# Last down projection as seven products of Strassen's form

## The chip, the cores and the metric

The kernel runs on one core of a Trainium2 chip. A core has a matrix engine (TensorE, PE in the profile; its weight loads are PEld), a vector engine (VectorE, DVE), a scalar engine (ScalarE, ACT), a general engine (GpSimd, POOL) and a sync engine (SyncE, SP) that issues the transfers here. Each has a queue of its own that runs in order. Sixteen DMA engines carry the transfers. SBUF is the working memory; PSUM has eight banks of 128 x 512 float32 in which matmuls accumulate. The metric is the time of one execution on the device in microseconds (us), by the median of several.

## The reference, cut to what matters

Two layers over 1024 tokens of 1024 channels, in float32. Each layer is a token mixer and then a gated feed-forward with a short causal convolution. The change touches the last matrix product of the second layer.

```
D_MODEL = 1024; SEQ = 1024; FFN_DIM = 2816; FFN_CONV_WIDTH = 3
def conv_ffn(h, w_up, w_dw, b_dw, w_down):
    u = h @ w_up
    u = causal_dwconv(u, w_dw) + b_dw
    gate, val = jnp.split(u, 2, axis=-1)
    return (jax.nn.silu(gate) * val) @ w_down
...
    for i in range(DEPTH):
...
        h = rms_norm(x, ffn_norm_g[i])
        x = x + conv_ffn(h, ffn_w_up[i], ffn_w_dw[i], ffn_b_dw[i], ffn_w_down[i])
```

The down projection multiplies a 1024 x 2816 matrix (tokens by channels, called the activations below) by a 2816 x 1024 weight.

## The kernel before, in words

**Precision.** A float32 operand is split into a high part (a cast, L347, on ACT) and a low part (the operand minus the high part, L348, on DVE or POOL). `mm3` (L350) makes a product of three matmuls: high by high, high by low, low by high, at L353, L355 and L354. High and low parts stand in tiles `whi` and `wlo`, eight buffers each (`SPLIT_BUFS`, L46).

**Pieces.** The work is a stream of `Piece` objects (L62): each may have a load, a split and a run (its matmuls or adds). `trace` (L259) writes them out: loads as far ahead as eight `raw` buffers allow, splits as long as the tiles of split pieces that have not run stay within `READY + 1` = 6 (a down piece has 2). The frame then orders each engine's queue by its own model of times, except PE's, which keeps the order of the pieces in this stage (`T.order(PE)`, in `ffn_up`, L1402). Waits between engines come from the data and from buffers that are used again.

**The up stage of the second layer** (`up`, L538) already computes its products in Strassen's form, as 2 x 2 blocks over halves of tokens, channels and columns. For each of 22 channel tiles f it runs products over PSUM banks y and z; the conv taps (L580), the gate (L589) and sums over blocks (L558 on POOL; L628, L638, L639, L643, L652 on DVE) follow. The result, 128 channels x 1024 tokens, is stored to `actd[f]` in HBM. Its factors stand in quarters of 128 x 4 x 512 (`quarter`, L156), eight in the pool `ht` and six in `late`.

**The down stage** (`down`, L408, called by `down_acts`, L691, and `ffn_down`, L1429) runs over the two halves h of the tokens and, in each, the two halves nh of the columns. For each of these four blocks it takes four PSUM banks (128 tokens x 512 columns each) and goes over the 22 channel tiles: a piece loads `actd[f]` for 512 tokens and 512 columns of the weight's rows, 256 KB each, splits both, and makes 4 x 3 matmuls of 128 x 512. After the 22 pieces a piece adds the four banks to the residual (L435), and after the second half of the columns a row block of 128 x 1024 is stored to the output (`out`, L1506). That is 88 pieces and 1056 matmuls. The residual is fetched from HBM after the fourth piece (`fetch_x`, L1296). The first two down pieces stand between the last up pieces (`STOP` in `up`).

**Buffers near the change.** `bank` (L505) takes one of six PSUM banks; two more are in the pool `pst`. `part` (L405) takes one of 14 tiles of 128 x 512.

Of the kernel before, what the change touches and what calls it, by code (L numbers as in the profile page):

```python
# [9 lines left out]
F32 = mybir.dt.float32  # L10
# [3 lines left out]
ALU = mybir.AluOpType  # L14
# [3 lines left out]
P = 128  # L18
# [7 lines left out]
NF = F // P  # L26
# [3 lines left out]
def f32(ap):  # L30
    return ap.bitcast(F32)
# [13 lines left out]
RAW_BUFS = 8  # L45
# [27 lines left out]
class Weight:  # L73
# [6 lines left out]
    def load(self):  # L80
        if self.raws:
            self.raw = self.t.load(self.src, self.shape)

    def split(self):
        t = self.t
        if not self.raws:
            self.parts = tuple(
                t.wp.tile(self.shape, F32R, tag=m, name=t.n(m), bufs=SPLIT_BUFS) for m in ("whi", "wlo")
            )
            for part, src in zip(self.parts, (self.hi, self.lo)):  # L90
                t.nc.sync.dma_start(f32(part), src)
# [21 lines left out]
class Trunk:  # L113
# [577 lines left out]
    def down_acts(self, xs, l, h, actd, w_down, after, los=None, actlo=None):  # L691


        def act(f, w):
            src = actd[f][:, h * 512 : (h + 1) * 512]
            if actlo and f in actlo:
                return Weight(self, None, [P, 512], actlo[f], hi=src)
            return Weight(self, src, [P, 512], vector=w.lo is None)

        rows = [w_down[l, f * P : (f + 1) * P, :] for f in range(NF)]  # L700
        for nh in range(2):
            yield from self.down(xs, h, nh, act, rows, after if nh == 1 else None, los)


    def attn(self, wst0, x_in, gain, w_in, b_f, q_g, k_g, extra=lambda *a: None, early=lambda: None):
# [599 lines left out]
def trunk(ctx, tc, a):  # L1305
    nc = tc.nc
    T = Trunk(ctx, tc)
# [32 lines left out]
    actd = [dram.tile([P, S], F32, name=f"actd{f}") for f in range(NF)]  # L1340
    xds = [[dram.tile([P, D], F32, name=f"xd{i}_{t}") for t in range(NB)] for i in range(3)]
# [4 lines left out]
    xs = [None] * NB  # L1346
# [36 lines left out]
    def turned(gen, n=1):  # L1383

        for i in range(6):
            yield T.norms(int(i < 4), int(1 <= i < 5), int(i >= 2))
            yield from some(gen, (1 if i else LAG) * n)
# [14 lines left out]
    def ffn_up(l, keep, first, then, late, fac, ups, held=()):  # L1402


        keep["vector"] = True
        if late:
            yield from turned(first)
        combine = T.combine(fac, keep)
        for _ in range(6):
            yield from some(combine, 1)  # L1410
            yield from some(first, 1 if late else 2)
        for i in range(6):
            yield from some(combine, 1)
            yield from some(first, 1)
            if i >= 6 - BEFORE:
                if held:
                    yield held.pop(0)
                else:
                    yield from some(ups, 1)
        keep["stop"] = True  # L1420
        yield from first
        yield T.order(PE)
        for p in ups:
            if p is STOP:
                yield from some(then, 1)
            else:
                yield p

    def ffn_down(l, h, xd, after, los=None, actlo=None):  # L1429
        for i, p in enumerate(T.down_acts(xs, l, h, actd, a["ffn_w_down"], after, los, actlo)):  # L1430
            yield p
            if i == 3:
                yield Piece(lambda: T.fetch_x(xs, xd, h))

    keep = {"xd": xds[0]}
# [17 lines left out]
    for ct in range(KT):  # L1453
        for s in range(2):
            for q in range(2):
                c0 = s * D + ct * P
                src = w_pw1.rearrange("(k p) n -> p k n", p=P)[:, 4 * q : 4 * q + 4, c0 : c0 + P]
                T.ahead.append(lambda src=src, lo=pwlo[2 * ct + s][q]: T.split_ahead(src, lo))
    for f in range(NF):
        for nh in range(2):  # L1460
            src = a["ffn_w_down"][0, f * P : (f + 1) * P, nh * 512 : (nh + 1) * 512]
# [7 lines left out]
    keep1 = {"xd": xds[2]}  # L1469
# [33 lines left out]
        return T.conv(xs, xds[1], h, hc, w_pw1, pwlo, taps, vec, a["conv_w_pw2"][0], halo,  # L1503
                      normer(grows, keep1, True))

    def out(tb):  # L1506
        nc.sync.dma_start(a["out"][0, tb * P : (tb + 1) * P, :], xs[tb])

    PE = mybir.EngineType.PE

    def pieces():
        conv_rows = ((grows, a["conv_norm_g"][0]), (b2, a["conv_b_pw2"][0]))
        yield T.order()
        down0 = ffn_down(0, 0, xds[0], conv_norm)
        yield from ffn_up(0, keep, T.early(0, keep, w_up), down0, False, *ups_of(0, keep))
        yield T.order()
        for r in conv_rows:
            yield fetch(*r)
        while (yield from some(down0, ASIDE)):
            if T.ahead:  # L1520
                yield T.ahead.pop(0)()
        down1 = ffn_down(0, 1, xds[0], conv_norm, dnlo, actlo)
        yield from turned(down1)
        main0, norm0, rest0 = conv(0)
        yield from main0([down1])
        yield from some(down1, 3)
        yield from some(norm0, 1)
        yield from some(down1, 3)
        yield from both(norm0, down1, 1, 2)
        for r in conv_rows:  # L1530
            yield fetch(*r)
# [12 lines left out]
        yield from turned(main1, 2)  # L1544
        first = T.early(1, keep1, w_up)
        fill.append(first)
        yield from main1
        yield T.order()
        keep1["vector"] = True
        yield from some(first, 5)  # L1550
        yield from some(norm1, 1)
        yield from some(first, 3)
        keep1["hold"] = True
        while keep1["begun"]:
            yield from some(norm1, 1)
            yield from some(first, 1)
        keep1["hold"] = False
        yield fetch(grows, a["ffn_norm_g"][1])
        fac, ups = ups_of(1, keep1)
        held = []  # L1560
        yield from norm1
        yield from some(rest1, 8)
        for p in itertools.islice(ups, 3):
            ahead, then = T.apart(p)
            yield ahead
            held.append(then)
        yield from rest1
        downs = [ffn_down(1, h, xds[2], out) for h in range(2)]
        yield from ffn_up(1, keep1, first, downs[0], True, fac, ups, held)
        for d in downs:  # L1570
            yield from d

    T.trace(pieces())


# [23 lines left out]
```

## Time and profile before

| what | us |
|---|---|
| median of three runs | 2324.36 |
| lowest and highest | 2323.95, 2328.08 |
| the profiled execution, by the device | 2321.22 |
| its span, first to last instruction | 2319.5 |
| first matmul of the last down projection | 2068.1 |
| its last matmul starts | 2312.7 |

The profile is of one execution. A row of a group shows an engine, an operation, the tiles it writes and reads, and its busy time. Where three numbers stand with slashes, they are the least, the median and the greatest duration in nanoseconds. In a timeline a row begins with the start and the duration in us, and a bracket shows how long the engine was idle before it and what ended that. Rows by stretches of the span show the busy time of each engine in each. PE's matmuls overlap: a matmul of 128 x 512 is shown with 389 ns, but one starts every 227 ns.

### The profile page before, as it was taken

The numbers are of one execution on the slowest core, as the hardware profiler recorded it, in microseconds if no ns is written. First come the engines' busy times: TensorE is split into PE (matmuls) and PEld (weight loads), VectorE is DVE, ScalarE is ACT, GpSimd is POOL, SyncE is SP. The second block draws the span as 40 slices with busy tenths as digits, with TensorE's granted clock in tenths as the row PEclk, the third lists the DMA queues.
The fourth block names the chain that finished last, engine by engine and source line by source line (L and its number), as shares of the span: only waits on it lengthen the run. The fifth ranks groups of instructions, "written<-read, shape, count | busy, mean of one in ns | idle before, by whom it ended". The sixth has DMA issues, their size and how long they took to land.

```text
span 2319.5 us, 35294 instructions
## 1 busy us (share of the span) xinstructions
PE 2252.0 (97%) x11282; PEld 1927.3 (83%) x11282; DVE 1648.1 (71%) x2751; ACT 1358.0 (59%) x2835; POOL 1406.7 (61%) x1191
## 2 busy tenths in 40 slices
PE   7899999998999999999999999998999999999998
PEld 7899999997878887777787887787877788888887
DVE  6567777777367999998436995699639999983222
ACT  5566666667255666666545665566635666664443
POOL 3445555535017988886554886677536999955543
PEclk9999999999999999999999999999999999999999
DMA  5222222134155546666878767654564554566664
GB/s 146 65 78 83 78 78 78 57 127 166 66 178 188 154 151 207 198 200 199 300 250 296 249 226 263 217 185 142 166 202 154 156 154 150 154 224 208 221 202 153
DMA packets 366841, 392.63 MB, mean 169 GB/s; under 512 B 26416, under 2 KB 245312, under 8 KB 366656
## 3 DMA queue, kind: packets, MB, share of 16 engines
q1 hardware_dynamic: 366656, 390.38, 53.2%
q8 instruction: 89, 1.46, 0.3%
q14 instruction: 96, 0.79, 0.1%
HBM read 299.78 MB, written 82.12 MB: 165 GB/s over the span
## 4 chain that ended last, share of the span: by engine, by line
PE 47%; DVE 17%; issue 4%; ACT 3%; DMA 1%; POOL 1%; SPq 0%; DVEq 0%; ACTq 0%; POOLq 0%
DVE acc L580 8%; PE dn L354 7%; PE dn L355 7%; PE dn L353 7%; PE pw L353 2%; PE pw L354 2%; PE pw L355 2%; PE e L353 2%; PE e L355 2%; PE e L354 2%; PE y L353 2%; PE y L354 1%; PE y L355 1%; ACT acc L584 1%; PE wops L353 1%
## 5 line engine op out<-in xcount | busy, mean ns | idle before, releaser
L348 POOL TENSOR_TENSOR wlo<-raw,whi 128x512 fp32r<-128x512 f32 (+1 forms) x306 | 444.8, 1456 | 275.2 <-ACT whi L347 239.3
L347 ACT CAST whi<-raw 128x512 fp32r<-128x512 f32 (+2 forms) x497 | 303.2, 633 | 263.9 <-PE dn L354 154.3
L348 DVE TENSOR_TENSOR wlo<-raw,whi 128x512 fp32r<-128x512 f32 (+1 forms) x191 | 149.3, 784 | 228.0 <-ACT whi L347 207.9
L348 POOL TENSOR_TENSOR wlo<-s,whi 128x512 fp32r<-128x512 f32 x176 | 258.8, 1480 | 64.1 <-ACT whi L347 64.1
L353 PE MATMUL dn<-whi,whi 128*128 128x512 f32 x704 | 275.7, 392 | 1.0 <-ACT whi L347 0.6
L354 PE MATMUL dn<-wlo,whi 128*128 128x512 f32 x704 | 274.6, 390 | 0.8 <-POOL wlo L348 0.8
L355 PE MATMUL dn<-whi,wlo 128*128 128x512 f32 x704 | 274.4, 390 | 0.0
L1182 DVE SCALAR_TENSOR_TENSOR cacc<-u,ctaps,cacc 128x512 f32<-128x512 f32 x320 | 238.6, 754 | 9.0
L1187 POOL TENSOR_TENSOR pacc<-pacc,prod 128x512 f32<-128x512 f32 x144 | 188.9, 1314 | 50.1 <-ACT prod L1186 43.8
L353 PE MATMUL y<-bhi,whi 128*128 128x512 f32 x528 | 207.6, 393 | 7.7 <-DVE u L638 5.2
L355 PE MATMUL y<-bhi,wlo 128*128 128x512 f32 x528 | 205.8, 390 | 0.0
L354 PE MATMUL y<-blo,whi 128*128 128x512 f32 x528 | 205.6, 389 | 0.0
L169 POOL TENSOR_SCALAR ss<-ss 128x4 f32<-128x4 f32 (+1 forms) x96 | 22.9, 238 | 289.9 <-ACT hn L189 150.2
L353 PE MATMUL pj<-whi,hthi 128*128 128x384 f32 (+1 forms) x512 | 177.8, 348 | 4.6 <-DVE zf L824 2.6
L355 PE MATMUL pj<-whi,htlo 128*128 128x384 f32 (+1 forms) x512 | 177.2, 346 | 0.0
L354 PE MATMUL pj<-wlo,hthi 128*128 128x384 f32 (+1 forms) x512 | 176.2, 344 | 0.7 <-DVE wlo L348 0.7
L558 POOL TENSOR_TENSOR s<-raw,raw 128x512 f32<-128x512 f32 x88 | 126.4, 1436 | 59.5 <-DMA c11d<-ev 58.2
L914 POOL TENSOR_SCALAR x<-x,nm 128x896 f32<-128x896 f32 (+7 forms) x128 | 101.4, 797 | 100.1 <-DVE nm L913 72.3
L353 PEld LDWEIGHTS dn<-whi,whi 128*128 128x128 f32 x704 | 132.5, 188 | 29.5 <-issue 1.1
L354 PEld LDWEIGHTS dn<-wlo,whi 128*128 128x128 f32 x704 | 132.6, 188 | 28.9 <-POOL wlo L348 1.2
L355 PEld LDWEIGHTS dn<-whi,wlo 128*128 128x128 f32 x704 | 132.5, 188 | 27.4
L584 ACT ACTIVATE acc<-acc 128x512 f32<-128x512 f32 x88 | 55.7, 632 | 163.3 <-DVE acc L580 162.4
(221 smaller groups left out, 6415.5 us busy)
## 6 DMA issues: line engine op xcount, KB each, us to landing
raw<-in_ffn_w_up_dram SPq DMA_DIRECT2D x240, 256.0 KB
raw<-in_ffn_w_down_dram SPq DMA_DIRECT2D x176, 256.0 KB
raw<-actd SPq DMA_DIRECT2D x152, 256.0 KB
raw<-in_conv_w_pw_dram SPq DMA_DIRECT2D x96, 256.0 KB
actd<-acc SPq DMA_DIRECT2D x76, 256.0 KB
wlo<-pwlo SPq DMA_DIRECT2D x64, 256.0 KB
raw<-in_fox_w_in_dram SPq DMA_DIRECT2D x64, 192.0 KB
xd<-x SPq DMA_DIRECT2D x24, 512.0 KB
```

Of the source, the lines that this page charges most:

```text
L169: nc.gpsimd.tensor_scalar(ss, ss, 1.0 / n, EPS, op0=ALU.mult, op1=ALU.add)
L347: self.nc.scalar.copy(hi, raw)
L348: (self.nc.vector if vector else self.nc.gpsimd).tensor_tensor(lo, raw, f32(hi), op=ALU.subtract)
L353: nc.tensor.matmul(out, lh, rh, start=start, stop=False, skip_group_check=more)
L354: nc.tensor.matmul(out, lh, rl, start=False, stop=False, skip_group_check=more)
L355: nc.tensor.matmul(out, ll, rh, start=False, stop=stop, skip_group_check=more)
L558: nc.gpsimd.tensor_tensor(st[o], *(st[m].rearrange("p a b -> p (a b)") if m[0] == "a" else st[m] for m in ((y, x) if o == "s4" else (x, y) ...
L580: nc.vector.scalar_tensor_tensor(acc[:, j:], ps[:, : 512 - j], tap[2 - j], acc[:, j:], op0=ALU.mult, op1=ALU.add)
L584: nc.scalar.activation(acc, acc, AF.Silu)
L914: nc.gpsimd.tensor_scalar(X[:, :L], X[:, :L], nm[:, 2:3], 1.0, op0=ALU.mult, op1=ALU.mult)
L1182: nc.vector.scalar_tensor_tensor(acc, win(j), tap(j), acc, op0=ALU.mult, op1=ALU.add)
L1187: nc.gpsimd.tensor_tensor(pacc, pacc, p, op=ALU.add)
```

## The change

The last layer's down projection is computed as seven products of 512 tokens x 1408 channels x 512 columns (Winograd's variant of Strassen's form) instead of eight. With a for blocks of the activations (first index tokens, second channels) and b for blocks of the weight (channels, columns):

- s2 = a21 + a22 − a11, t1 = b12 − b11, t2 = b22 − t1
- product 1 is a11 by b11, 2 is a12 by b21, 3 is (a12 − s2) by b22, 4 is a22 by (b21 − t2), 5 is (s2 + a11) by t1, 6 is s2 by t2, 7 is (a22 − s2) by (t2 − b11)

Each product has 11 pieces of 12 matmuls (77 pieces, 924 matmuls). They run two at a time, piece by piece: 1 and 6, 2 and 7, 5 and 4, then 3 alone. The banks are carried on: 2 accumulates onto the four banks of 1, then 7 and 4 onto those of 6, and 3 onto those of 5. Between, the banks are added to the residual: those of 1 to three blocks of the output (12 adds), and those of 6, 2, 7, 5, 4 and 3 to one each (4 adds). When an output block of 512 x 512 has its last add, it is stored in four pieces of 128 x 512.

The sums s2, t1 and t2 are kept in quarters; those of the pieces overwrite loaded tiles. `ALU` sums marked g run on POOL, those marked v on DVE. In `Weight(..., vector=True)` the low part is made on DVE, otherwise on POOL. Product 6 loads four tiles for each piece into `part` buffers, and products 1, 2, 7, 5, 4 and 3 load two, two, two, one, two and two into `raw` buffers; 1's two stay until 6 has used them for its sums. The residual of both halves is fetched after the fourth piece.

```
+    def down_seven(self, xs, xd, l, actd, w_down, out):
...
+        def add(eng, o, x, y, op, j):
+            eng.tensor_tensor(t[o, j], t[x, j], t[y, j], op=op)
+
+        def first_sums(j):
+            keep("s2", j), keep("t1", j), keep("t2", j)
+            add(v, "t1", "b12", "b11", ALU.subtract, j)
+            add(g, "s2", "a21", "a22", ALU.add, j)
+            add(v, "t2", "b22", "t1", ALU.subtract, j)
+            add(g, "s2", "s2", "a11", ALU.subtract, j)
...
+        plan = {
+            1: ("x", "a11 b11", None, ("a11", "b11"), (True, False)),
+            6: ("y", "a21 a22 b12 b22", first_sums, ("s2", "t2"), (True, True)),
+            2: ("x", "a12 b21", None, ("a12", "b21"), (True, False)),
+            7: ("y", "a22 b11", lambda j: (add(g, "a22", "a22", "s2", ALU.subtract, j),
+                                           add(v, "b11", "t2", "b11", ALU.subtract, j)), ("a22", "b11"), (True, False)),
+            5: ("z", "a11", lambda j: add(g, "a11", "s2", "a11", ALU.add, j), ("a11", "t1"), (True, False)),
+            4: ("y", "a22 b21", lambda j: add(v, "b21", "b21", "t2", ALU.subtract, j), ("a22", "b21"), (True, False)),
+            3: ("z", "a12 b22", lambda j: add(v, "a12", "a12", "s2", ALU.subtract, j), ("a12", "b22"), (True, False)),
+        }
...
+            def run():
+                if j == 0 and fresh:
+                    banks[ps] = [
+                        self.pst.tile([P, 512], F32, tag="t", name=self.n(ps)) if ps == "y" and b >= 2 else self.bank(ps)
+                        for b in range(4)
+                    ]
+                (hi, lo), right = w[0].parts, w[1].parts
+                for b in range(4):
+                    c = slice(b * P, (b + 1) * P)
+                    self.mm3(banks[ps][b], hi[:, c], lo[:, c], *right, fresh and j == 0, j == N - 1, not fresh)
+
+            raws, freed = {1: (2, 0), 6: (1, 3)}.get(n, (len(gets), len(gets)))
+            return Piece(run, load, split, raws, freed, tiles=2)
...
+                        v.tensor_tensor(xs[tb][:, m], xs[tb][:, m], banks[ps][b], op=ALU.add)
+                        if (i, c) == last:
+                            nc.sync.dma_start(out[tb * P : (tb + 1) * P, m], xs[tb][:, m])
...
+        def two(n, m, lag):
+            for j in range(N + lag):
+                if j < N:
+                    yield piece(n, j)
+                    if j == N - 1:
+                        yield n
+                if j >= lag:
+                    yield piece(m, j - lag)
+            yield m
+
+        sums = {
+            1: ("x", ((0, 1), (1, 0), (1, 1))), 6: ("y", ((0, 1),)), 2: ("x", ((0, 0),), (0, 0)),
+            7: ("y", ((1, 1),)), 5: ("z", ((1, 1),), (1, 1)), 4: ("y", ((1, 0),), (1, 0)),
+        }
+        count = 0
+        for n, m, lag in ((1, 6, 2), (2, 7, 1), (5, 4, 1)):
+            for p in two(n, m, lag):
+                yield gather(*sums[p]) if isinstance(p, int) else p
+                count += 1
+                if count == 4:
+                    yield Piece(lambda: [self.fetch_x(xs, xd, h) for h in range(2)])
+        for j in range(N):
+            yield piece(3, j)
+        yield gather("z", ((0, 1),), (0, 1))
...
-        downs = [ffn_down(1, h, xds[2], out) for h in range(2)]
-        yield from ffn_up(1, keep1, first, downs[0], True, fac, ups, held)
-        for d in downs:
-            yield from d
+        down = T.down_seven(xs, xds[2], 1, actd, a["ffn_w_down"], a["out"][0])
+        yield from ffn_up(1, keep1, first, down, True, fac, ups, held)
+        yield from down
```

More of the change, by code (lines that the diff above doesn't have):

```diff
@@ L702, in down_acts, with act, weight, keep @@
             yield from self.down(xs, h, nh, act, rows, after if nh == 1 else None, los)
+    def down_seven(self, xs, xd, l, actd, w_down, out):
+        nc = self.nc
+        v, g = nc.vector, nc.gpsimd
+        N = NF // 2
+        t, kept, banks = {}, {}, {}
+        def act(i, k):
+            return lambda j: actd[k * N + j][:, i * 512 : (i + 1) * 512]
+        def weight(k, c):
+            return lambda j: w_down[l, (k * N + j) * P : (k * N + j + 1) * P, c * 512 : (c + 1) * 512]
+        src = {f"{m}{i + 1}{k + 1}": of(i, k) for m, of in (("a", act), ("b", weight)) for i in range(2) for k in range(2)}
+        def keep(m, j):
+            if (m, j // 4) not in kept:
+                kept[m, j // 4] = self.quarter(m, F32, late=m == "t1" and j >= 8)
+            t[m, j] = kept[m, j // 4][:, j % 4, :]
+        def add(eng, o, x, y, op, j):
[16 more added lines that the diff above has]
+        }
+        def piece(n, j):
+            ps, gets, sums, names, vector = plan[n]
+            gets = gets.split()
+            fresh = n in (1, 6, 5)
+            w = [Weight(self, lambda m=m: t[m, j], [P, 512], vector=e) for m, e in zip(names, vector)]
+            def load():
+                for m in gets:
+                    if n == 6:
+                        t[m, j] = self.part(m)
+                    else:
+                        t[m, j] = self.wp.tile([P, 512], F32, tag="raw", name=self.n(m), bufs=RAW_BUFS)
+                    nc.sync.dma_start(t[m, j], src[m](j))
+            def split():
+                if sums:
+                    sums(j)
+                for x in w:
+                    x.split()
+            def run():
[10 more added lines that the diff above has]
+            return Piece(run, load, split, raws, freed, tiles=2)
+        def gather(ps, where, last=None):
+            def run():
+                for b in range(4):
+                    for i, c in where:
+                        m = slice(c * 512, (c + 1) * 512)
+                        tb = 4 * i + b
+                        v.tensor_tensor(xs[tb][:, m], xs[tb][:, m], banks[ps][b], op=ALU.add)
+                        if (i, c) == last:
+                            nc.sync.dma_start(out[tb * P : (tb + 1) * P, m], xs[tb][:, m])
+            return Piece(run)
+        def two(n, m, lag):
[21 more added lines that the diff above has]
+        yield gather("z", ((0, 1),), (0, 1))
@@ L1504, in conv @@
                       normer(grows, keep1, True))
-    def out(tb):
-        nc.sync.dma_start(a["out"][0, tb * P : (tb + 1) * P, :], xs[tb])
     PE = mybir.EngineType.PE
```

## The prediction

> **What bounds the kernel now.** I read the page's head first, then busy time by stretches of the span, then the tile view of the last down projection's banks, then the waits.
>
> ```profile
> span 2319.5 us, 35294 instructions
> PE 2252.0 (97%) x11282; PEld 1927.3 (83%) x11282; DVE 1648.1 (71%) x2751; ACT 1358.0 (59%) x2835; POOL 1406.7 (61%) x1191
> ```
>
> ```profile
> 1900.00:1950.00 50.00, 49.79 (x219) 40.60 (x218) 46.42 (x56) 31.26 (x69) 45.58 (x34) 1.00 0.50 150
> 2100.00:2150.00 50.00, 50.00 (x223) 41.39 (x222) 14.77 (x22) 20.87 (x37) 24.88 (x19) 1.00 0.64 192
> 2250.00:2300.00 50.00, 50.00 (x222) 41.39 (x221) 14.77 (x22) 21.26 (x38) 24.48 (x19) 1.00 0.58 179
> ```
>
> ```profile
> L353 PE MATMUL dn<-whi,whi x352: 389/389/389, 2068.1 to 2312.2; 128*128 128x512 f32 x176
> ```
>
> ```profile
> ACT whi L347 <- PE dn L354: 123.5, 79, 1.6
> ```
>
> The columns of the second fence are length, then PE, PEld, DVE, ACT and POOL busy, clock, DMA share, GB/s. In the stage that the change rewrites, PE is busy 50.00 of 50 us at the full clock, while DVE, ACT and POOL are busy under half the time. The casts on ACT wait for PE to give back operand buffers, so everything else is ahead of PE. This stage is bound by matmuls alone. The stage before it (1900:1950) is PE-bound too, but there POOL and DVE are over 90% busy.
>
> The pace: 352 starts of L353 with 8 from two up pieces among them make 359 steps in 2312.2 − 2068.1 = 244.1 us, so 0.680 us for three matmuls. A piece (12 matmuls) takes 2.72 us, the 88 pieces 239.4 us.
>
> **The change part by part.** *Matmuls.* 7 products of 11 pieces are 77 pieces instead of 88: 44 × 3 matmuls fewer, 44 × 0.680 = **29.9 us less**. Shape and operand types stay, so the pace should too.
>
> *Loads.* 165 tiles of 256 KB instead of 176, but unevenly: products 1 and 6 side by side load 6 tiles in each pair of pieces (5.44 us), 289 GB/s.
>
> ```profile
> 2060.00:2065.00 5.00, 5.00 (x24) 4.14 (x23) 3.90 (x7) 4.24 (x10) 2.62 (x2) 1.00 0.97 304
> 2075.00:2080.00 5.00, 5.00 (x24) 4.14 (x23) 4.76 (x7) 4.96 (x11) 1.03 (x1) 1.00 1.01 373
> ```
>
> Full queues moved 304 to 373 GB/s here (the residual's 4 MB are in it, at the same place after the change), so 289 fits, with little over. From the steady rows, 2 tiles in 2.72 us at a share of 0.64 cost 0.87 us each, 5.2 us for six. I take 0; the other end is the rival below.
>
> *Vector work.* Splits fall from 176 to 154, but 99 sums over whole tiles appear: 4 on POOL and 5 on DVE for each of 11 indices. By numbers there is room. But the two engines disturb each other:
>
> ```profile
> L580 DVE SCALAR_TENSOR_TENSOR acc<-x,ffntab,acc x30: 1301/1660/1843, 1852.4 to 2047.3; 128x511 f32<-128x511 f32 x15, 128x510 f32<-128x510 f32 x15
> L580 DVE SCALAR_TENSOR_TENSOR acc<-y,ffntab,acc x28: 736/746/752, 1857.4 to 2037.2; 128x511 f32<-128x511 f32 x14, 128x510 f32<-128x510 f32 x14
> L589 DVE TENSOR_TENSOR acc<-acc,acc x29: 692/1378/1476, 1849.8 to 2042.8; 128x512 f32<-128x512 f32 x29
> ```
>
> ```profile
> 2042.81 1.48 DVE L589 TENSOR_TENSOR acc<-acc,acc 128x512 f32<-128x512 f32 x1 [0.16 <-ACT acc L584]
> 2045.41 3.53 DVE L580 SCALAR_TENSOR_TENSOR acc<-x,ffntab,acc 128x511 f32<-128x511 f32 x2
> 2057.01 0.70 DVE L639 TENSOR_TENSOR c<-z,u 128x512 f32<-128x512 f32 x1
> 2057.62 0.68 DVE L589 TENSOR_TENSOR acc<-acc,acc 128x512 f32<-128x512 f32 x1
> 2058.22 0.69 DVE L628 TENSOR_TENSOR u<-y,p 128x512 f32<-128x512 f32 x1
> ```
>
> ```profile
> 2042.44 1.30 POOL L558 TENSOR_TENSOR s<-raw,raw 128x512 f32<-128x512 f32 x1
> 2046.65 1.74 POOL L348 TENSOR_TENSOR wlo<-s,whi 128x512 fp32r<-128x512 f32 x1
> 2048.35 1.74 POOL L558 TENSOR_TENSOR s<-raw,s 128x512 f32<-128x512 f32 x1
> 2050.05 2.55 POOL L348 TENSOR_TENSOR wlo<-s,whi 128x512 fp32r<-128x512 f32 x2
> ```
>
> The first fence: the same DVE operation takes 0.75 us when its input is in PSUM (y) and 1.66 us when both tensors are in SBUF (x, fetched). In the timelines DVE's L589 starts at 2042.81 under a POOL operation that ends at 2043.74, and ends at 2044.29, 0.55 us after it. So a DVE operation on two SBUF tensors and a POOL operation exclude each other. Call them D and G. Alternating, one D and one G take 1.70 us (POOL starts 2046.65, 2048.35, 2050.05); G alone takes 1.25 (two in 2.55, less the overlap) and D alone 0.60 (starts 2057.01, 2057.62, 2058.22).
>
> Count D and G by pair of pieces, each against 5.44 us of PE:
> - 1 with 6: D 5 (two sums, three low parts), G 3 (two sums, one low part): 3 × 1.70 + 2 × 0.60 = 6.30 us.
> - 2 with 7, and 5 with 4: D 3, G 3: 5.10 us.
> - 3 alone, against 2.72: D 2, G 1: 2.30 us.
>
> Over 11 indices that is 206.8 us against PE's 209.5. Products 1 and 6 are no longer bound by PE: 69.3 us against 59.8, **9.5 us more**. The others fit at 94%. The up stage shows that such a load can be kept up: for each f, 4 D (two L580 on x, two L589) and 9 G come to 4 × 1.70 + 5 × 1.25 = 13.05 us in 13.6 (96%), and PE was busy 49.79 of 50. So I take 0.5 us for these 22 pairs.
>
> [...]
>
> *Adds.* Banks are added 36 times instead of 16. After product 1 twelve adds follow at once, after 6 four more.
>
> ```profile
> 2311.08 2.73 DVE L435 TENSOR_TENSOR x<-x,dn 128x512 f32<-128x512 f32 x4 [7.66 <-PE dn L355]
> 2311.80 2.78 SPq L1507 DMA_DIRECT2D out_dram<-x  x4
> ```
>
> Starts are 0.61 to 0.68 us apart: 12 × 0.61 = 7.4 us. They wait for the last matmul of product 1, the low parts and sums of 6's last two pieces stand about them in DVE's queue, and product 2 cannot write a bank before its three adds. Three pieces of PE (8.2 us) lie between, which would hide them on a free DVE; here DVE is what is short. The later adds, four each with two pieces before the banks' next use, stay hidden (2.5 of 5.4 us).
>
> *The start.* The six banks of the main pool go to product 1 (four) and 6 (two, beside both banks of the small pool). The last of them holds z of the final up pair.
>
> ```profile
> 2082.43 0.69 DVE L652 TENSOR_TENSOR z<-z,u 128x512 f32<-128x512 f32 x1
> 2085.93 0.74 DVE L580 SCALAR_TENSOR_TENSOR acc<-z,ffntab,acc 128x510 f32<-128x510 f32 x1
> ```
>
> It is read until 2086.67. Piece 6.0 is the sixth from 2068.1 and reaches its second bank at 2068.1 + 5 × 2.72 + 0.68 = 2082.4: it waits 4.3 us. D and G go on meanwhile.
>
> *Sum for products 1 and 6.* 9.5 + 7.4 = 16.9 us late, less what was ahead. Splits run three pieces ahead, 8.2 us, of which a piece needs 3.2 (two casts 1.14, low parts 0.69 and 1.34):
>
> ```profile
> 2098.73 0.69 DVE L348 TENSOR_TENSOR wlo<-raw,whi 128x512 fp32r<-128x512 f32 x1 [2.03 <-ACT whi L347]
> ```
>
> ```profile
> 2099.23 1.34 POOL L348 TENSOR_TENSOR wlo<-raw,whi 128x512 fp32r<-128x512 f32 x1 [1.39 <-ACT whi L347]
> ```
>
> ```profile
> 2098.01 1.14 ACT L347 CAST whi<-raw 128x512 fp32r<-128x512 f32 x2 [1.58 <-PE dn L354]
> ```
>
> That leaves 5.0 us: **11.9 us lost**. The wait for z lies inside it. Ends: 0, if sums run far enough ahead (parts for three indices fit), and 9.5 + 7.4 + 4.3 = 21.2, if nothing is ahead and all add up. I take 11.9, since the up stage's own tail keeps DVE busy while the lead would have to be built.
>
> *The end.* Four adds as before, but the last stores are 256 KB instead of 512.
>
> ```profile
> 2314.00:2316.00 2.00, 0.00 (x0) 0.00 (x0) 0.00 (x0) 0.00 (x0) 0.00 (x0) 0.97 1.03 422
> 2316.00:2318.00 2.00, 0.00 (x0) 0.00 (x0) 0.00 (x0) 0.00 (x0) 0.00 (x0) 0.50 0.82 336
> ```
>
> The stores fill the DMAs after the last add. Half of 2.1 MB at 422 GB/s is 2.5 us; since the last add and issue stay, I take **1.8 us less** (ends 0 and 2.5).
>
> The sum: −29.9 + 11.9 + 0.5 − 1.8 = −19.3 us. The profiled execution took 2321.2 us (1.7 beside its span), so 2301.9; the median is 3.1 above it, so **2305.0 us**.
>
> **The rivals.**
> [...]
> - *Loads bind first:* 66 tiles at 0.87 and the residual (8 × 512 KB, 11 us at 373 GB/s) are 68.5 us, some 6 beyond PE after what was loaded early: 2324.4 − 29.9 + 6 − 1.8 = 2298.7. For it: a share of 1.01 at 2075. Against: full queues passed 373 GB/s.
> [...]
> - *Slower: queue order.* DVE and POOL run in a fixed order. If sums wait behind low parts that wait for casts, which wait for PE's buffers, the exclusion stands idle. At 206.8 us of work the change breaks even when the stage takes 239.4 + 1.8 = 241.2, 14% idle; at 20% it takes 258.5, **2342 us**. For it: a product-6 piece is a chain over POOL twice, ACT and DVE. Against: the up stage has the same chain.
> - *Not what it says:* were the seven products not 924 matmuls, or planned elsewhere, nothing would be gained: 2324. The diff speaks against it.
>
> **How the numbers follow.** Forecast (2300 to 2312) 0.52, no stall 0.12, loads 0.10, dearer exclusion 0.16 (2313 to 2326), slower 0.08, not done 0.02. 0.2% (4.6 us) is about what a measurement can tell from no change. Faster: 0.52 + 0.12 + 0.10 and most of the dearer case, 0.84; same 0.09; slower 0.07. The range leaves out half of no stall, a part of the dearer case and the slower one: 2294 to 2319.
>
> **What would show it.** Right: 924 matmuls 0.227 us apart, PE idle in products 1 and 6 only, waiting for low parts, by some 12 us; DVE's sums there at 1.3 to 1.8 us; then pairs of 5.44 us. A DMA share of 1 with waits for raw tiles would say loads; PE gaps on into products 7, 4 and 3 the dearer exclusion or the queues' order. Wrong would be a first pair without gaps, or a stage longer than 239 us.

## The result and the profile after

| | before | after |
|---|---|---|
| median, us (9 runs each) | 2323.62 | 2331.96 |
| lowest and highest | 2320.19, 2328.08 | 2330.61, 2335.28 |
| span of the profiled execution | 2319.5 | 2328.9 |
| first matmul of the down stage | 2068.1 | 2076.7 |
| start of its last matmul | 2312.7 | 2324.9 |

The ratio after to before is 1.0037 [1.0027, 1.0048]: the change makes the kernel 8.3 us slower. Forecast were 2305.0 us and a range of 2294 to 2319.

The head of the page of after, with span, busy time and instructions:

```profile
span 2328.9 us, 35049 instructions
PE 2238.6 (96%) x11150; PEld 1908.3 (82%) x11150; DVE 1754.3 (75%) x2826; ACT 1346.0 (58%) x2813; POOL 1454.0 (62%) x1213
```

The groups of the high-by-high matmuls of the down stage, one for each of its three sets of banks:

```profile
L353 PE MATMUL y<-whi,whi x132: 387/389/632, 2090.3 to 2294.5; 128*128 128x512 f32 x132
...
L353 PE MATMUL x<-whi,whi x88: 387/389/628, 2076.7 to 2224.0; 128*128 128x512 f32 x88
...
L353 PE MATMUL z<-whi,whi x88: 389/389/628, 2230.9 to 2324.4; 128*128 128x512 f32 x88
```

They are 308, and PE has 132 matmuls fewer in all: the products were made as the diff says, 924 matmuls, and 29.9 us of matmul time went. PE lost more than that in waiting. Busy time by stretches of after (length, then PE, PEld, DVE, ACT and POOL busy, clock, DMA share, GB/s):

```profile
2060.00:2070.00 10.00, 6.70 (x19) 5.36 (x20) 8.16 (x13) 3.71 (x7) 4.52 (x4) 0.66 0.68 225
2070.00:2130.00 60.00, 51.13 (x217) 39.64 (x216) 57.82 (x55) 27.97 (x57) 40.37 (x27) 1.00 0.84 293
2130.00:2145.00 15.00, 14.36 (x55) 11.09 (x54) 14.97 (x15) 4.66 (x8) 9.49 (x6) 0.89 0.44 152
2145.00:2295.00 150.00, 138.62 (x579) 110.70 (x578) 104.47 (x108) 55.41 (x96) 101.91 (x68) 0.97 0.48 154
```

Where before had PE at 50 of 50 us, PE now idles again and again up to 2245, in the first two thirds of the stage. From 2070 to 2145 (products 1 and 6) DVE is busy 96% of the time and more. After 2145 it is busy 70%, POOL 68% and the DMAs 48%: nothing is full, and still PE stands 11.4 us. And the clock, 1.00 in all of this stage before, falls below 1 in places.

To see the loss by stage, take the time from the first matmul of one pair of products to the first of the next, and subtract 0.2267 us for each matmul between. "Start" is the same sum from 2030 to the first matmul of product 1; before has 0.3 there.

| us lost | start | 1 and 6 | 2 and 7 | 5 and 4 | 3 |
|---|---|---|---|---|---|
| after | 7.4 | 14.2 | 14.8 | 4.5 | 0.0 |

That is 40.9 − 0.3 = 40.6 us lost. Gained are 29.9 us of matmuls and 2.8 at the end (from the last matmul's start to the end of the span, 6.8 before and 4.0 now): 7.9 us slower. Of the 9.4 us between the two spans, 1.9 are there at 2045 already, in work that both kernels share.

**The start.** DVE's timeline in after, and PE's at the same place:

```profile
2048.17 0.70 DVE L643 TENSOR_TENSOR y<-y,p 128x512 f32<-128x512 f32 x1 [0.83 <-PE y L355]
2053.04 1.05 DVE L728 TENSOR_TENSOR t<-b,b 128x512 f32<-128x512 f32 x1 [4.17 <-DMA b<-in_ffn_w_down_dram]
2054.01 1.78 DVE L580 SCALAR_TENSOR_TENSOR acc<-x,ffntab,acc 128x511 f32<-128x511 f32 x1
...
2062.48 0.67 DVE L638 TENSOR_TENSOR u<-y,p 128x512 f32<-128x512 f32 x1
```

```profile
2063.30 0.76 PE L353 MATMUL y<-bhi,whi 128*128 128x512 f32 x1 [4.29 <-DVE u L638]
```

The first sum of product 6 (t1, L728) stands in DVE's queue ahead of the up stage's taps. Its weight tile is not there yet, so DVE idles for 4.17 us with the taps behind it. They reach u 4 us late, u gives back the bank y late, and PE waits 4.29 us in the up stage. Most of the rest of the 7.4 is the clock, 0.50 from 2061.61 to 2068.44 (last section).

**Products 1 and 6.** Durations (least, median, greatest, in ns) of DVE's and POOL's operations of after between 2060 and 2300, the low parts first, then sums:

```profile
L348 DVE TENSOR_TENSOR wlo<-a,whi x58: 674/1752/1783, 2064.9 to 2299.3; 128x512 fp32r<-128x512 f32 x58
L348 POOL TENSOR_TENSOR wlo<-b,whi x49: 1261/1600/2463, 2059.3 to 2299.1; 128x512 fp32r<-128x512 f32 x49
```

```profile
L728 POOL TENSOR_TENSOR s<-s,a x11: 1594/1627/1744, 2060.7 to 2138.5; 128x512 f32<-128x512 f32 x11
L728 DVE TENSOR_TENSOR t<-b,t x10: 677/1714/1774, 2090.0 to 2143.8; 128x512 f32<-128x512 f32 x10
```

DVE needs 0.68 us where POOL is still and 1.75 where POOL works. In the stretch 2070:2130 above, 55 operations fill 57.82 us of DVE.

**Products 2 and 7.** One turn of it in the timeline of after:

```profile
2181.48 1.28 POOL L728 TENSOR_TENSOR a<-a,s 128x512 f32<-128x512 f32 x1 [3.42 <-DMA a<-actd]
...
2182.72 2.94 POOL L348 TENSOR_TENSOR wlo<-b,whi 128x512 fp32r<-128x512 f32 x2
...
2182.99 1.53 DVE L728 TENSOR_TENSOR b<-t,b 128x512 f32<-128x512 f32 x1 [3.78 <-DMA b<-in_ffn_w_down_dram]
2184.00 0.33 SPq L761 DMA_DIRECT2D b<-in_ffn_w_down_dram  x1
...
2184.03 0.50 PE L354 MATMUL x<-wlo,whi 128*128 128x512 f32 x1 [1.88 <-POOL wlo L348]
```

And what POOL, SP's queue and PE waited for between 2150 and 2215 (us in all, times, longest):

```profile
POOL a L728 <- DMA a<-actd: 17.3, 6, 3.6
```

```profile
SPq L761 <- POOL wlo L348: 36.8, 13, 5.4
SPq L761 <- DVE wlo L348: 15.1, 8, 3.8
```

```profile
PE x L354 <- POOL wlo L348: 5.9, 4, 2.2
```

PE waits for the low part of b21 (product 2). That low part waits in POOL's queue behind product 7's sum a22 − s2. The sum waits for its tile a22. The tile's load waits in SP's queue for a raw buffer. And raw buffers come free with low parts: SP issues the weight at 2184.00, as soon as POOL has done the first of its two, and the next a22, which stands behind that weight in SP's queue, at 2186.24, after a low part of DVE. Over the whole pair (2156 to 2231) PE waits 8.3 us in five pieces for POOL's low parts, and slow matmuls behind two of them add 2.8 (last section), together most of the 14.8. So three queues that run in order wait for each other in a ring, while no engine and no transfer is at its limit.

### The profile page after: what moved, and what is told of

It reads as the page before. It is cut to its first block, busy times and chain, and to the rows that moved or that the text cites. A ratio compares the mean times of both kernels' runs of the same rounds, so it can differ in the third digit from the quotient of the medians.

```text
span 2328.9 us, 35049 instructions
## 1 busy us (share of the span) xinstructions
PE 2238.6 (96%) x11150; PEld 1908.3 (82%) x11150; DVE 1754.3 (75%) x2826; ACT 1346.0 (58%) x2813; POOL 1454.0 (62%) x1213
## 4 chain that ended last, share of the span: by engine, by line
PE 39%; DVE 21%; issue 5%; DMA 5%; ACT 4%; POOL 1%; SPq 0%; DVEq 0%; ACTq 0%; POOLq 0%
DVE acc L580 9%; PE dn L354 4%; PE dn L355 4%; PE dn L353 4%; PE pw L353 2%; PE pw L355 2%; PE pw L354 2%; PE y L353 2%; PE e L353 2%; DMA b<-in_ffn_w_down_dram 2%; PE e L354 2%; PE e L355 2%; DVE wlo L348 2%; PE y L354 2%; PE y L355 2%
## 5 line engine op out<-in xcount | busy, mean ns | idle before, releaser
L348 POOL TENSOR_TENSOR wlo<-raw,whi 128x512 fp32r<-128x512 f32 (+1 forms) x218 | 323.9, 1488 | 150.5 <-ACT whi L347 132.8
L347 ACT CAST whi<-raw 128x512 fp32r<-128x512 f32 (+2 forms) x321 | 202.2, 640 | 140.3 <-PE dn L354 35.7
L348 DVE TENSOR_TENSOR wlo<-raw,whi 128x512 fp32r<-128x512 f32 (+1 forms) x103 | 84.6, 826 | 79.0 <-ACT whi L347 68.2
L353 PE MATMUL dn<-whi,whi 128*128 128x512 f32 x352 | 139.1, 395 | 1.4 <-ACT whi L347 1.0
L354 PE MATMUL dn<-wlo,whi 128*128 128x512 f32 x352 | 138.5, 394 | 0.9 <-POOL wlo L348 0.9
L355 PE MATMUL dn<-whi,wlo 128*128 128x512 f32 x352 | 138.3, 393 | 0.0
L347 ACT CAST whi<-s 128x512 fp32r<-128x512 f32 x187 | 111.7, 615 | 44.8 <-PE y L354 16.8
L353 PE MATMUL z<-bhi,whi 128*128 128x512 f32 x352 | 137.0, 389 | 0.0
L354 PE MATMUL z<-blo,whi 128*128 128x512 f32 x352 | 136.9, 389 | 0.0
```

The lines of the kernel that those rows point to most:

```text
L347: self.nc.scalar.copy(hi, raw)
L348: (self.nc.vector if vector else self.nc.gpsimd).tensor_tensor(lo, raw, f32(hi), op=ALU.subtract)
L353: nc.tensor.matmul(out, lh, rh, start=start, stop=False, skip_group_check=more)
L354: nc.tensor.matmul(out, lh, rl, start=False, stop=False, skip_group_check=more)
L355: nc.tensor.matmul(out, ll, rh, start=False, stop=stop, skip_group_check=more)
```

## The experiments

They tell apart three accounts of the loss. **Exclusion**: D (a DVE operation on two SBUF tensors) and G (a POOL operation) shut each other out, and the pairs cost what the prediction's counts say. **Queues**: sums, low parts and loads wait for each other in fixed orders. **Lead**: what is late in 2 and 7 is a debt of 1 and 6. All ratios are to the kernel before, measured beside. All losses by stage:

| us | median | ratio | start | 1, 6 | 2, 7 | 5, 4 | 3 |
|---|---|---|---|---|---|---|---|
| all sums and low parts on DVE | 2301.65 | 0.9909 [0.9894, 0.9923] | 7.3 | 3.2 | 1.8 | 0.0 | 0.0 |
| more buffers | 2330.89 | 1.0032 [1.002, 1.0044] | 6.5 | 19.3 | 10.0 | 4.5 | 0.0 |
| both | 2310.28 | 0.9942 [0.9926, 0.9959] | 7.5 | 4.6 | 7.3 | 0.1 | 0.0 |
| lag 3 | 2330.25 | 1.0028 [1.0019, 1.0037] | 0.3 | 22.7 | 15.9 | 4.4 | 0.0 |
| all DVE, lag 3 | 2300.72 | 0.9912 [0.99, 0.9925] | 1.9 | 8.5 | 0.0 | 0.0 | 0.0 |
| DVE's low parts by ACT | 2315.96 | 0.997 [0.996, 0.9981] | 6.9 | 12.6 | 3.0 | 1.4 | 0.0 |
| sums on DVE | 2315.57 | 0.997 [0.9957, 0.9982] | 7.0 | 17.0 | 0.0 | 2.4 | 0.1 |
| low parts on DVE | 2314.52 | 0.9968 [0.9956, 0.998] | 7.7 | 13.4 | 1.3 | 2.8 | 0.0 |
| DVE in 1 and 6 | 2316.93 | 0.9981 [0.9972, 0.9991] | 6.7 | 4.9 | 13.4 | 1.4 | 0.6 |
| DVE in the rest | 2311.92 | 0.9958 [0.9943, 0.9973] | 7.1 | 14.4 | 1.5 | 0.0 | 0.0 |
| DVE in 1 and 6, more buffers | 2316.72 | 0.9982 [0.9972, 0.9991] | 7.1 | 3.3 | 13.7 | 4.5 | 0.0 |
| all DVE, lag 3, residual set later | 2298.94 | 0.9902 [0.9888, 0.9917] | 1.9 | 8.1 | 0.0 | 0.0 | 0.0 |
| same load, no POOL sum in 7 | 2309.87 | 0.9941 [0.9921, 0.996] | 7.5 | 5.0 | 5.3 | 2.2 | 1.1 |
| same load, no loads in 7 | 2308.77 | 0.9929 [0.9912, 0.9946] | 6.4 | 3.3 | 7.0 | 0.0 | 1.1 |

A row's losses less 33.0 us (29.9 + 2.8 + 0.3) give its median against before to within 3 us, so the table holds nearly the whole effect. The losses are those of one profiled execution, the medians those of 4 to 10, and executions of one kernel lie up to 15 us apart ("sums on DVE": 2306.41 to 2321.18). So two or three us between two rows say little. Of each of the last two kernels the profiled execution was the slowest of four.

**First four: engine, buffers, lag.** Everything to DVE:

```
-        v, g = nc.vector, nc.gpsimd
+        v = g = nc.vector
-            1: ("x", "a11 b11", None, ("a11", "b11"), (True, False)),
+            1: ("x", "a11 b11", None, ("a11", "b11"), (True, True)),
...
```

(and so for products 2, 7, 5, 4 and 3)

> All sums and low parts of the seven products on DVE, none on POOL; buffers, loads and pieces as in the change. Changed kernel: 2332 us, PE lost 14.2 us in products 1 and 6, 14.8 in 2 and 7, 4.5 in 5 and 4, and 7.4 before the first piece. Exclusion theory: a POOL operation costs the pair of engines 1.15 us where the same on DVE costs 0.60, so the load falls to 4.8 of 5.44 us in 1 and 6 and to 3.6 in the later pairs; DVE's sums return to 0.7 us; losses fall to about 7, 3 and 1 us, time about 2312. Raw-buffer theory (a load waits until a low part gives a raw buffer back, the sums wait for the load): the losses in 2 and 7 shrink only by what the shorter low part saves, stay above 8 us, time about 2322 or more. Queue-order theory: losses stay, 2330.

2301.65 us, 21.1 below before, some 30 below the change and 10 below the lowest of the three forecasts. Durations and stretches of this kernel:

```profile
L348 DVE TENSOR_TENSOR wlo<-a,whi x65: 673/686/695, 2065.1 to 2286.1; 128x512 fp32r<-128x512 f32 x65
```

```profile
2070.00:2130.00 60.00, 57.28 (x252) 46.88 (x251) 56.71 (x93) 31.67 (x61) 1.30 (x1) 1.00 0.88 321
2130.00:2145.00 15.00, 15.00 (x67) 12.20 (x66) 15.00 (x26) 6.07 (x11) 0.00 (x0) 1.00 0.13 43
2145.00:2295.00 150.00, 148.50 (x655) 122.86 (x655) 113.74 (x185) 59.09 (x104) 0.00 (x0) 1.00 0.56 181
```

With POOL idle, DVE does 93 operations in the stretch in which it did 55, at 0.69 us instead of 1.75. Taking work from an engine that was two thirds busy and giving it to the one that was 96% busy took 28.6 us of the losses away (40.9 to 12.3): a pair of 1 and 6 is 8 × 0.60 = 4.8 us of DVE now, in place of 6.30 for both.

Products 7 and 4 load into part tiles of their own, so that their loads need no raw buffer:

```
-                    if n == 6:
+                    if n in (6, 7, 4):
...
-            raws, freed = {1: (2, 0), 6: (1, 3)}.get(n, (len(gets), len(gets)))
+            raws, freed = {1: (2, 0), 6: (1, 3), 7: (0, 0), 4: (0, 0)}.get(n, (len(gets), len(gets)))
```

> Only the two loads of products 7 and 4 go to part buffers (free after product 6) instead of raw buffers, so loads of the later pairs can run further ahead. Exclusion theory: nothing but waits of sums for loads changes, the losses in 2 and 7 and in 5 and 4 stay at 12 to 19 us, time 2328 to 2332. Raw-buffer theory: those 19 us fall to 4 or less, waits of sums for loads go, time about 2316. Products 1 and 6 and the stretch before the first piece are untouched in both (14 and 7 us).

2330.89 us, as the change. Products 2 and 7 lose 4.8 us less, 1 and 6 5.1 more. Both edits together:

> Both edits: all on DVE, and part buffers for 7 and 4. If each cause has its own share, this is the sum of the two gains against the changed kernel; if the exclusion alone decides, it equals the kernel with all on DVE (about 2312); if the raw buffers alone decide, it equals the kernel with more buffers. Both theories with all gains: losses about 7 us in 1 and 6, 1 in the rest, time about 2309.

2310.28 us, 8.6 above DVE alone: 2 and 7 lose 7.3 us in place of 1.8. So a lack of buffers as such is not the cause. Why this one is worse than DVE alone was not followed up.

Product 6 three pieces behind product 1 in place of two, which moves its first sums away from the up stage's end:

```
-        for n, m, lag in ((1, 6, 2), (2, 7, 1), (5, 4, 1)):
+        for n, m, lag in ((1, 6, 3), (2, 7, 1), (5, 4, 1)):
```

> Product 6 runs three pieces behind product 1 instead of two. Theory on the start: the first sum t1 stands in DVE's queue before the up stage's last taps and waits there 4.2 us for its load, which holds a PSUM bank and stops PE for 4.45 us, and PE then runs 2.9 us longer at half clock. If so, with the first sums needed later, the 7.4 us lost before the first piece fall to 2 or less, time about 2326. Rival: the order of loads does not change with the pieces' order, the loss stays and the time is 2331 to 2333.

The stall at the start is gone (0.3 us), as the account of its cause said, but 1 and 6 give it back: 22.7 us in place of 14.2, so the 2326 us forecast with it did not come (2330.25). What DVE doesn't do early it has to do later, and later it is short.

**Second four: which part of the work.** DVE alone with lag 3:

> All sums and low parts on DVE, and product 6 three pieces behind product 1. With all on DVE the later losses were 5 us and the stretch before the first piece still lost 7.3; with the lag alone that stretch lost 0.25, but products 1 and 6 lost 8.5 more. If products 1 and 6 could not use the earlier start because the exclusion bound them, then here, where it does not, the gain stays: 7 us less than all on DVE, about 2295. If the lag itself costs buffers, products 1 and 6 lose the 7 us again, about 2302.

2300.72 us, not told apart from lag 2 (2301.65): again start and 1 and 6 trade (7.3 + 3.2 against 1.9 + 8.5). DVE is full in 1 and 6, as its stretches show:

```profile
2090.00:2120.00 30.00, 26.63 (x110) 19.90 (x109) 29.67 (x50) 12.49 (x22) 0.00 (x0) 1.00 1.03 381
2120.00:2145.00 25.00, 23.62 (x105) 19.24 (x104) 25.00 (x42) 10.08 (x18) 0.00 (x0) 1.00 0.40 143
```

DVE's low parts left out, a second copy on ACT in their place, POOL's work as in the change:

```
                 for x in w:
-                    x.split()
+                    if not x.vector:
+                        x.split()
+                        continue
+                    raw = x.src()
...
+                    for m in x.parts:
+                        nc.scalar.copy(m, raw)
```

> The low parts that DVE makes (of the left operands, and t2) are replaced by a plain copy of the operand on ACT: the difference is left out of the computation. POOL keeps all its sums and low parts, in the same pieces. Exclusion theory: DVE now has 2 operations on two SBUF tensors per index in products 1 and 6 and 1 later, so POOL runs at 1.25 us and the load of the pair of engines is 4.65 and 4.2 of 5.44 us: the losses (14.2, 14.8, 4.5) fall to under 6, 4 and 1. Theory that POOL's slower operations and their order in its queue are the cause without the exclusion: the losses in 2 and 7 stay over 10 us. ACT gets 3 more copies per pair, 4.3 of 5.44 us busy, which could cost a little in both.

Only the sums on DVE (the first line of the first diff), POOL's low parts as in the change:

> Only the four sums that POOL made go to DVE; POOL keeps its low parts. Load by the exclusion: products 1 and 6 one G and seven D, 1.70 + 6 x 0.60 = 5.3 of 5.44 us; 2 and 7, and 5 and 4, two G and four D, 4.6. Exclusion theory: losses between the change and all on DVE, about 7 in 1 and 6 and 4 in 2 and 7, time about 2312. Queue-order theory (sums stand in POOL's queue behind low parts that wait for PE's buffers): the losses in 2 and 7 go wholly, as with all on DVE.

Only the low parts on DVE (the other lines of it), POOL's sums as in the change:

> Only the low parts that POOL made go to DVE; POOL keeps its sums. Load by the exclusion: products 1 and 6 two G and six D, 2 x 1.70 + 4 x 0.60 = 5.8 of 5.44 us; 2 and 7, and 5 and 4, one G and five D, 4.1. Exclusion theory: some 4 to 8 us lost in 1 and 6, under 3 in 2 and 7, time about 2308. Queue-order theory: no sum waits behind a low part on POOL, so also 1 and 6 lose no more than with all on DVE (3 us), time about 2302.

All three come to 2314.5 to 2316.0 us, above every time forecast for the last two. By the prediction's counts (1.70 for a D with a G, 1.25 and 0.60 alone) a pair of 2 and 7 takes 4.2, 4.6 and 4.1 us in them, in place of 5.10, and loses 3.0, 0.0 and 1.3 in place of 14.8. The 0.0 is what the account by queues said for the kernel with the sums on DVE. But a pair of 1 and 6 takes 4.65, 5.30 and 5.80, and all three lose 12.6 to 17.0 there, far more than was expected (under 6, about 7, 4 to 8). Two of the three counts are under the 5.44 us of PE, so it isn't the load alone. With DVE's low parts gone, nearly all of the loss is one wait of 9.8 us and the slow matmuls behind it. Timelines of DVE and PE in that kernel:

```profile
2100.84 1.60 DVE L728 TENSOR_TENSOR t<-b,b 128x512 f32<-128x512 f32 x1 [5.48 <-DMA b<-in_ffn_w_down_dram]
...
2104.03 0.74 DVE L580 SCALAR_TENSOR_TENSOR acc<-z,ffntab,acc 128x510 f32<-128x510 f32 x1
```

```profile
2104.92 0.77 PE L353 MATMUL y<-whi,whi 128*128 128x512 f32 x1 [9.82 <-DVE acc L580]
```

This is the second bank of piece 6.0, which holds z of the last up pair: the taps that read z stand in DVE's queue behind a sum that waits 5.48 us for its weight. It is the stall at the start over again, at another bank. With the sums on DVE there are two waits, 6.3 us at that bank, and this one (DVE, POOL and PE):

```profile
2120.65 0.68 DVE L348 TENSOR_TENSOR wlo<-t,whi 128x512 fp32r<-128x512 f32 x1
2121.25 0.68 DVE L728 TENSOR_TENSOR s<-a,a 128x512 f32<-128x512 f32 x1
...
2131.49 0.68 DVE L728 TENSOR_TENSOR t<-b,t 128x512 f32<-128x512 f32 x1
```

```profile
2120.90 13.61 POOL L348 TENSOR_TENSOR wlo<-b,whi 128x512 fp32r<-128x512 f32 x2 [3.74 <-ACT whi L347]
```

```profile
2133.34 0.79 PE L354 MATMUL x<-wlo,whi 128*128 128x512 f32 x1 [5.08 <-POOL wlo L348]
```

And its group of POOL's low parts (least, median, greatest):

```profile
L348 POOL TENSOR_TENSOR wlo<-b,whi x53: 1262/1395/12382, 2067.6 to 2298.5; 128x512 fp32r<-128x512 f32 x53
```

DVE runs 19 operations 0.60 us apart without a break, and POOL, which started the first of two low parts at 2120.90, ends it 12.38 us later, when DVE's run is over. The two engines don't take turns there; POOL is shut out.

**Third four: a debt, or the pair itself?** DVE alone for products 1 and 6, the rest as in the change:

```
-            add(g, "s2", "a21", "a22", ALU.add, j)
+            add(v, "s2", "a21", "a22", ALU.add, j)
...
-            1: ("x", "a11 b11", None, ("a11", "b11"), (True, False)),
+            1: ("x", "a11 b11", None, ("a11", "b11"), (True, True)),
```

(and so for the second sum of s2)

> Sums and low parts of products 1 and 6 on DVE; products 2, 7, 5, 4 and 3 use POOL as in the change, 5.10 of 5.44 us of the pair of engines. Lead theory: 2 and 7 lost 14.8 us in the change because products 1 and 6 left no split piece ahead; with 3 us lost in 1 and 6 the lead is there and 5.10 holds, as it did in the up stage, so 2 and 7 lose under 4, 5 and 4 under 2, time about 2305. Load theory: 94% cannot be held whatever comes before, 2 and 7 lose 10 or more, time 2313 or more.

1 and 6 fall from 14.2 to 4.9, 2 and 7 lose 13.4, as before. So 2 and 7 owe nothing to 1 and 6: the lead theory falls. The reverse:

> The reverse: products 1 and 6 use POOL as in the change (6.30 of 5.44 us), all later ones DVE alone (3.6). Both theories: 14 us lost in 1 and 6 as in the change, under 2 after, 7 before the first piece, time about 2314. If the losses in 1 and 6 come from what follows, they would fall.

14.4 and 1.5. The two parts add up. With part tiles for products 7 and 4 beside DVE in 1 and 6:

> As with DVE in 1 and 6, and products 7 and 4 load into part buffers. Raw-buffer theory: if 2 and 7 lose 10 us or more with DVE in 1 and 6 alone, they lose under 4 here. Load theory: no difference between the two. With all on DVE the same buffers cost 6 us in 2 and 7 (order of loads); if that is general, this one is the slower.

13.7 in 2 and 7: these buffers don't help, and they don't open the ring of queues either. Between 2145 and 2215 SP's queue still waits 43.1 us for POOL's low parts and 16.5 for DVE's, and POOL's sums wait 14.6 for a22; which buffer each load waited for was not followed. And the best kernel so far (DVE alone, lag 3) with the residual's load after 14 pieces in place of 4:

```
-                if count == 4:
+                if count == 14:
```

> All on DVE, three pieces between 1 and 6 (8.5 us lost in 1 and 6, DMA share 1.02 from 2090 to 2120), and the 4 MB of the residual fetched after the fourteenth piece instead of the fourth. If loads bind products 1 and 6 there, the loss falls by 3 us or more, time about 2297. If DVE binds them (10.00 busy in 10 us), nothing changes, 2300. If the frame fetches the residual as early as before, the DMA share tells it.

2298.94 us, not told apart from the two others with DVE alone. But this did not move the loads. SP's issues of the residual (L1417) in this kernel, and then in the one with count 4:

```profile
2059.18 0.32 SPq L1417 DMA_DIRECT2D x<-xd  x1
...
2071.58 1.74 SPq L1417 DMA_DIRECT2D x<-xd  x4
```

```profile
2058.00 0.35 SPq L1417 DMA_DIRECT2D x<-xd  x1
...
2070.39 1.74 SPq L1417 DMA_DIRECT2D x<-xd  x4
```

The frame put them at the same place of SP's queue, 1.2 us later as is the whole stage, and the DMA share from 2090 to 2120 is 1.05 where it was 1.03. So this run repeats the kernel before it and says nothing on the residual. What stands is that DVE is full there (29.67 of 30 us above), beside DMAs that are full too (share 1.03, 381 GB/s).

**Last two: load or ring in 2 and 7?** Both have DVE alone in 1 and 6, and the same count of 3 D and 3 G in a pair of 2 and 7. In the first the sum a22 − s2 goes to DVE, and for it the low part of a12 goes to POOL, so that POOL makes both of product 2:

```
-            2: ("x", "a12 b21", None, ("a12", "b21"), (True, False)),
-            7: ("y", "a22 b11", lambda j: (add(g, "a22", "a22", "s2", ALU.subtract, j),
+            2: ("x", "a12 b21", None, ("a12", "b21"), (False, False)),
+            7: ("y", "a22 b11", lambda j: (add(v, "a22", "a22", "s2", ALU.subtract, j),
```

> As with DVE in products 1 and 6, but in 2 and 7 the sum of a22 moves from POOL to DVE and the low part of a12 from DVE to POOL: the load of the pair of engines stays at three G and three D, 5.10 of 5.44 us. Load theory (94% of the exclusion cannot be held here): 2 and 7 lose 10 us or more as before (13.4). Queue-loop theory (the sum on POOL waits for its load ahead of a low part whose end frees the buffer for the next load): 2 and 7 lose under 4.

The frame then orders the queues anew, so more than the sum's place can differ. In the second the engines make the same sums and low parts in 2 and 7 as in the change, and from 2165 to 2192 POOL and DVE do so in the same order as in "DVE in 1 and 6". But product 7 loads nothing; its sums read s2 and t2, so the kernel does not compute product 7:

```
-            7: ("y", "a22 b11", lambda j: (add(g, "a22", "a22", "s2", ALU.subtract, j),
-                                           add(v, "b11", "t2", "b11", ALU.subtract, j)), ("a22", "b11"), (True, False)),
+            7: ("y", "a22 b11", lambda j: (add(g, "a22", "t2", "s2", ALU.subtract, j),
+                                           add(v, "b11", "t2", "s2", ALU.subtract, j)), ("a22", "b11"), (True, False)),
...
-                    nc.sync.dma_start(t[m, j], src[m](j))
+                    if n != 7:
+                        nc.sync.dma_start(t[m, j], src[m](j))
```

> As with DVE in products 1 and 6, but product 7's two loads are left out and its sums read s2 and t2, which are in SBUF: the same engines make as many sums and low parts, 5.10 of 5.44 us, only the loads and the waits for them are gone (product 7 is not what the reference needs). Load theory: 2 and 7 still lose 10 us or more. Queue-loop theory: under 4.

The same 50 us of "DVE in 1 and 6", and then of these two:

```profile
2150.00:2200.00 50.00, 43.00 (x184) 33.65 (x183) 30.14 (x24) 17.98 (x31) 31.68 (x22) 1.00 0.45 147
```

```profile
2150.00:2200.00 50.00, 50.00 (x221) 41.01 (x220) 28.71 (x31) 20.13 (x35) 34.84 (x26) 1.00 0.53 173
```

```profile
2150.00:2200.00 50.00, 49.94 (x221) 41.00 (x220) 38.52 (x30) 19.42 (x35) 43.51 (x29) 1.00 0.26 89
```

At the same load PE goes from 43.00 to 50.00 of 50 us, with 221 matmuls for 184, when the sum that waits for a load leaves POOL's queue, and as much when the loads are gone. So most of what 2 and 7 lost is the ring of queues: 13.4 becomes 5.3 and 7.0. The other 5 to 7 us come at the end of the pair in both (from 2200 on), and whether load or order makes them stays open. That shorter operations open the ring too is not shown as cleanly. The kernel with DVE's low parts by ACT keeps POOL's queue as it is and loses 3.0 us, but with DVE's low parts it also loses one of the things that SP waits for. The two others (0.0 and 1.3 us) each take a link out of POOL's queue. So the exclusion makes each turn longer and the order makes it a ring, but their shares are not told apart.

## Why the prediction was wrong

- **Matmuls: right.** 924 of them, 29.9 us less.
- **Exclusion: right, by what it cost.** D took 0.68 us without POOL and 1.75 with it. Six kernels that keep POOL out of 1 and 6 at lag 2 lose 3.2 to 5.0 us there; those that leave it a share lose 12.6 to 22.7. The 12.38 us of one POOL operation, beside 19 DVE operations 0.60 us apart, show more than the count has: one G lasted through a whole stream of D. The chance of a dearer exclusion (0.16, 2313 to 2326 us) was the author's estimate: no run shows the figures behind its times, and what the runs showed is 1.70 us for a D with a G and, at times, single POOL operations of 8.04 and 12.38 us. The case of no stall (0.12) did not come either: the change lost 14.2 us in 1 and 6.
- **Products 1 and 6: near in sum, 11.9 forecast and 14.2 found, but partly by luck.** By the gaps between PE's starts, waits for DVE's low parts before 2140 cost 8.1 us, against 9.5 for the load. The wait at 6.0's second bank came and cost 2.8, where 4.3 were worked out and counted as lying inside the sum. The clock took 1.6. But the adds after product 1 (2149 to 2156), forecast at 7.4, cost one wait of 0.9 at most: they ran beside product 6's last pieces. That excess and the 5.0 us of lead taken off nearly cancel. DVE busy 57.82 of 60 us fits the load. But the two kernels with a smaller load and larger waits there say that the order on DVE's queue could have made such a loss without the load.
- **The step that failed** is the one on 2 with 7 and 5 with 4: "The up stage shows that such a load can be kept up (…) So I take 0.5 us for these 22 pairs." They lost 14.8 + 4.5 = 19.3 us, 18.8 more than the term, and that alone takes the time out of the range. Of the sign that was named for a dearer exclusion or the order of queues, PE gaps on into products 7, 4 and 3, the first two came. A count of 94% says that the work fits, not that the queues let it run: at the same count the loss was 13.4, 7.0 or 5.3 us, by what stood ahead of the low part and what that waited for. The up stage was an example of the count and not of the order. Why 5 with 4, at the same 5.10 us, lost only 4.5 was not tried; it loads three tiles in a pair where 2 with 7 load four, which may be it.
- **The start: not foreseen.** The working looked at the bank of z and not at what the first sums of product 6 do to the up stage's own work behind them in DVE's queue: 7.1 us. It is worth less than that, since without it 1 and 6 lose it again.
- **The clock: not foreseen.** About 8.5 of the 40.6 us are matmuls at half rate after gaps, 0.43 us apart in place of 0.23.
- **The end:** 2.8 us saved where 1.8 was taken. **Loads**, taken at 0, were not tested in 1 and 6, since the residual's loads did not move. In the change DVE waits 0.9 us for loads there and POOL's sums 7.3 (2077 to 2156), and PE's waits are for DVE, which is full; that speaks for the 0 but does not show it.
- The rival "slower: queue order" had the right kind and sign. It put the wait at casts; it was at loads. It had a chance of 0.08, because the up stage "has the same chain", the same mistake as above.

The gain was there to be had: with all sums and low parts on DVE, the 33 us of matmuls and end come through but for 10 to 12, and the kernel takes 2299 to 2302 us, 21 to 22 below before. With the share that the change leaves to POOL all of it is lost.

## What to carry to other kernels

Where two engines shut each other out, count the cost of a pair, not of an engine: giving the "free" engine an operation here cost the pair 1.10 to 1.25 us (1.70 − 0.60, or alone) where the busy one would have done it in 0.60. A load under 100% is necessary and not enough (at 94% 2 with 7 lost 14.8 us here); before taking a stage as covered, write down for each in-order queue (SP's too) what stands ahead of the operation that the bound engine needs and what that waits for, and look for a ring through buffers. An operation of a new stage that is set into a queue early, ahead of its data, stalls the old stage behind it: here DVE stood 4.17 and 5.48 us, and PE behind it 4.29 and 9.82.

## What the runs showed of the hardware

**A gap on PE can cost more than its length.** PE's timeline in after, behind a wait of 2.84 us:

```profile
2128.90 0.50 PE L354 MATMUL y<-wlo,whi 128*128 128x512 f32 x1 [2.84 <-DVE wlo L348]
...
2129.99 0.63 PE L355 MATMUL y<-whi,wlo 128*128 128x512 f32 x1
2130.41 0.63 PE L353 MATMUL y<-whi,whi 128*128 128x512 f32 x1
...
2133.59 0.40 PE L355 MATMUL x<-whi,wlo 128*128 128x512 f32 x1
2133.82 0.40 PE L353 MATMUL x<-whi,whi 128*128 128x512 f32 x1
```

From 2129.9 the starts are 0.43 us apart in place of 0.23, for 3.41 us, then at full rate again. The granted clock is 0.50 from 2129.88 to 2133.29, and 1.00 from 2068.44 to 2129.87 and from 2133.30 to 2184.40. In after this happened at 2061.6 (6.83 us long), 2129.9, 2184.5, 2222.0 and 2242.5, the first time within a wait of 4.29 us and then 0.5 to 1.0 us behind waits of 2.84, 1.88, 2.45 and 2.22 us; 44 matmuls fell into it, 8.5 us. The four later ones begin 68.27, 122.88, 160.43 and 180.91 us after the first by the clock record of this trace, near 20, 36, 47 and 53 times the 3.41 us of one such stretch; why was not shown. But after waits of 2.63 us (to 2093.77) and 2.19 us (to 2206.07) the clock stayed at 1.00, so in these the length of a wait alone did not decide it. What did was not tried.

**DVE and POOL don't always take turns.** Where both have work, one D and one G often alternate, some 1.70 us for both, as POOL and DVE in the kernel with the low parts on DVE:

```profile
2120.97 1.62 POOL L728 TENSOR_TENSOR s<-s,a 128x512 f32<-128x512 f32 x1
2122.56 1.73 POOL L728 TENSOR_TENSOR s<-a,a 128x512 f32<-128x512 f32 x1
2124.36 1.62 POOL L728 TENSOR_TENSOR s<-s,a 128x512 f32<-128x512 f32 x1
```

```profile
2121.36 1.78 DVE L348 TENSOR_TENSOR wlo<-s,whi 128x512 fp32r<-128x512 f32 x1
2123.07 1.77 DVE L348 TENSOR_TENSOR wlo<-t,whi 128x512 fp32r<-128x512 f32 x1
```

But the 12.38 us above, and this POOL operation of the kernel with DVE in 1 and 6, show it waiting for a whole run of DVE operations 0.60 us apart (11 start within its 8.04 us):

```profile
2128.16 8.04 POOL L728 TENSOR_TENSOR a<-a,s 128x512 f32<-128x512 f32 x1 [57.32 <-DMA a<-actd]
```

What decides between the two was not tried.
